# The second layer's attention: products with the values of two units in one chunk, and where the preparations of keys and values stand

## The chip, the cores and the metric

The kernel runs on one core of one Trainium2 chip. The metric is the device time of one execution in microseconds, the median of several runs. A core has five engines that work through queues of their own and wait for each other by semaphores: TensorE (PE in the profile, matmuls and transposes), VectorE (DVE), ScalarE (ACT), GpSimd (POOL) and SyncE (SP, which issues DMAs).

## The reference

The program is a backbone of two layers over 1024 latent tokens and 256 context tokens, 1024 wide. The first layer is windowed attention beside a gated MLP. The second, which matters here, is latent attention with 16 heads: queries from a rank of 256, keys and values from a rank of 128, a rotary part of 32 shared by all heads' keys, and a gate.

```python
def mla_keys_values(kv_a, k_pe, kv_norm, w_kvb, row, col):
    kv = (rms_norm(kv_a, kv_norm) @ w_kvb).reshape(B_, L, C_HEADS, C_NOPE + C_V)
    k_nope, v = kv[..., :C_NOPE], kv[..., C_NOPE:]
    ...
    k = jnp.concatenate([k_nope, jnp.broadcast_to(k_pe, (B_, L, C_HEADS, C_ROPE))], axis=-1)
    return k, v

    ...
    def one(qblk):
        s = jnp.einsum('bqhd,bkhd->bhqk', qblk, k).astype(jnp.float32) * scale
        p = jax.nn.softmax(s, axis=-1).astype(v.dtype)
        return jnp.einsum('bhqk,bkhd->bqhd', p, v)

    ...
    y = (o * jax.nn.silu(gate)) @ w_out
```

All is float32. Each latent token attends to all 1280 tokens.

## The kernel before

The first layer, the second layer's projections and the output products stand before and after the part that changes, and are not touched. In `layer1_attention` the work is cut into 64 units `(hp, qg, e)`: 8 pairs of heads, 4 groups of 256 queries, 2 heads of a pair. The even and the odd unit of the same `hp` and `qg` are the two heads of a pair; their results share one accumulator in PSUM. A loop over n = 0 to 66 runs one step each, and inside a step the list `ORDER1` (line 43) gives the order of the operations by letters. The order of PE, ACT, DVE and POOL is exactly the order in which the program writes them (`manual_schedule`, line 1319); only DMAs on SP are placed by the planner.

What the letters do in step n:

- S0 to S4 (`scores`): scores of unit n, each as three matmuls in a split of float32 in two parts. S0 and S1 fill the two-bank tile s0 (first 128 queries, 1024 keys), S2 and S3 the tile s1 (other 128 queries), S4 the context's 256 keys of both (`sx`).
- X0, X1, X2 (`maxima`, DVE) and P0, P1 (`peak`, DVE): the largest score of each row.
- E0 to E3 (`exponent`, ACT): exponentials and their sums. E0 and E2 are of the first 128 queries, E1 and E3 of the others.
- T0 to T4 (`turn`): transposes of the probabilities of unit n - 1 on PE, four at a time into one bank, and the copy out of that bank: T0 and T3 by DVE, T1, T2 and T4 by ACT (`TURNS`, line 45).
- A0 (`av`, line 1260): products of the transposed probabilities `pt` with the values, for both heads of pair m, keys `k0` to `k1` of ten blocks of 128. The two heads go to the two halves of 64 columns of PE. `AVS` (line 44) says which blocks: in an even step n = 2m + 2 blocks 0 to 4, in the odd step n = 2m + 3 blocks 5 to 9.
- I and U (`inverses`, `inverses_out`): inverses of the sums, turned by PE into the same accumulator, in odd steps. C (`gated`): division and gate of a finished pair, by DVE, in the next even step.
- B and R (`prep_q`, in even steps): at B the queries' projection for the next group on PE, at R the casts to `qh` (ACT) and the subtractions to `ql` (DVE, line 1165) that empty its bank.
- D and L: one stage each of the preparations that `plan` (line 1304) picks for the step, by s = n mod 16: `prep_pair` (keys of the next pair of heads and weights of its queries) in the steps of `PAIR`, `prep_v` (values of the next four heads) in the steps of `VALUES` (line 41). The first step of each loads and splits weights; in the later ones D is the products on PE and L the copies out of PSUM. Keys come in three blocks of columns (512, 512, 256), values in five.

The banks of PSUM set what waits for what. `tm` is two banks in turn (line 1193), for the transposes T, the preparations' products and the queries' projection alike: each of these waits until the operation two before it in that row has been copied out. `acc` is one bank. The transposed probabilities `pt` have three buffers (`PTS`, line 28).

The list of line 43, with the tuples that the change touches:

```python
PAIR, VALUES = (2, 3, 4, 5, 8, 9, 11, 13), (1, 6, 7, 10, 12, 14)
ORDER1 = 'S0 S1 T0 T1 I C X0 S4 S2 X2 P0 T2 T3 E0 E2 S3 T4 D X1 P1 L E3 E1 A0 U B R'.split()
AVS = ((0, 5),), ((5, 10),)
TURNS = 'VAAVA'
```

Of the kernel before, what the change touches and what calls it, by code (L numbers as in the profile page):

```python
# [37 lines left out]
LAGS = 2, 1, 2, 3, 3  # L38
OUT_K = (3, 0, 1, 2, 4, 5, 6, 7)

PAIR, VALUES = (2, 3, 4, 5, 8, 9, 11, 13), (1, 6, 7, 10, 12, 14)
WQ = 'VGG'
ORDER1 = 'S0 S1 T0 T1 I C X0 S4 S2 X2 P0 T2 T3 E0 E2 S3 T4 D X1 P1 L E3 E1 A0 U B R'.split()
AVS = ((0, 5),), ((5, 10),)
TURNS = 'VAAVA'
KPE = {3: [0], 5: [1]}
KPEE = "AV"
# [6 lines left out]
class Kernel:  # L54
# [1116 lines left out]
    def layer1_attention(self):  # L1171
# [70 lines left out]
        def turn(n, a):  # L1242

            if a == 0:
                pts[n] = self.t(pp, [P, NT, QG], F32, "pt")
            tp = self.bank()
            blocks = [(k, j) for k in (8, 9) for j in range(2)] if a == 4 else [(4 * (a % 2) + k, a // 2) for k in range(4)]
            for o, (k, j) in enumerate(blocks):
                nc.tensor.transpose(tp[:, o * P:(o + 1) * P], probs[n][j][:, k * P:(k + 1) * P], self.ident)  # L1249
            if a == 4:  # L1250
                dst, src = pts[n][:, 8:10], tp.rearrange("p (k q) -> p k q", k=2)
            else:
                k, j = blocks[0]
                dst, src = pts[n][:, k:k + 4, j * P:(j + 1) * P], tp.rearrange("p (k q) -> p k q", k=4)
            if TURNS[a] == "A":
                nc.scalar.copy(dst, src)  # L1256
            else:
                nc.vector.tensor_copy(dst, src)  # L1258

        def av(m, k0, k1):  # L1260
            hp, qg, _ = units[2 * m]
            if k0 == 0:
                accs[m] = self.psum("acc")
            for kt in range(k0, k1):
                for e in range(2):
                    vc = ((2 * hp + e) % 4) * 64
                    mm(accs[m][64 * e:64 * e + 64, 0:QG], lhsT=self.v4[hp // 2][:, kt, vc:vc + 64],  # L1267
                       rhs=pts[2 * m + e][:, kt], start=kt == 0, stop=kt == NT - 1)

        def inverses(m):  # L1270

            t = totals.pop(m)
            nc.vector.tensor_tensor(t[:, 2], t[:, 0], t[:, 1], op=ALU.add)
            spread[m] = v = self.t(c2, [P, 2, 2, 64], F32, "spread", bufs=2)
            nc.vector.reciprocal(t[:, 2], t[:, 2])
            nc.gpsimd.tensor_copy(v, t[:, 2].rearrange("p (e j) -> p j e", e=2).unsqueeze(3).broadcast_to([P, 2, 2, 64]))

        def inverses_out(m):

            r = spread.pop(m).rearrange("p j e c -> p j (e c)")  # L1280
            for j in range(2):
                nc.tensor.transpose(accs[m][:, QG + j * P:QG + (j + 1) * P], r[:, j], self.ident)

        def gated(m):

            hp, qg, _ = units[2 * m]
            acc = accs.pop(m)
            cols = slice(qg * QG, (qg + 1) * QG)
            gt = self.t(k2, [P, QG], F32, "gt", bufs=2)
            nc.sync.dma_start(gt, self.g1_d[hp * P:(hp + 1) * P, cols])  # L1290
            nc.vector.scalar_tensor_tensor(gt, acc[:, QG:2 * QG], 0.5, gt, op0=ALU.mult, op1=ALU.mult)
            y = self.t(k2, [P, QG], F32, "y7", bufs=4) if hp == 7 else gt
            nc.vector.tensor_tensor(y, acc[:, 0:QG], gt, op=ALU.mult)
            if hp == 7:
                self.y7[qg] = y
            else:
                nc.sync.dma_start(self.c_d[qg, hp], y)

        def plan_q(n):
            hp, g = n // 8, n % 8 // 2 + 1  # L1300
            hp, g = (hp + 1, 0) if g == 4 else (hp, g)
            return [self.prep_q(hp, g)] if n % 2 == 0 and hp < 8 else []

        def plan(n):
            s, hp = n % 16, n // 8
            if s == 0:
                self.values = self.prep_v(hp // 2 + 1) if hp < 6 else iter(())
            if s % 8 == 0 and hp < 7:
                self.pairs = self.prep_pair(hp + 1)
            out = []  # L1310
            if s in PAIR and hp < 7:
                out.append(self.pairs)
            if s in VALUES:
                out.append(self.values)
            return out
# [3 lines left out]
        with self.tc.manual_schedule(engines={E.PE, E.Activation, E.DVE, E.Pool}):  # L1319
            for n in range(N + 3):  # L1320
                odd = n % 2
                for op in ORDER1:
                    o, a = op[0], int(op[1:] or 0)
                    if o in "SXPE":
                        if n < N:
                            {"S": scores, "X": maxima, "P": peak, "E": exponent}[o](n, a)
                    elif o == "T":
                        if 1 <= n <= N:
                            turn(n - 1, a)
                            if n == N and a in (1, 2, 3):  # L1330
                                next(first)
                    elif o in "AIU":

                        m = (n - 2 - odd) // 2
                        if 0 <= m < N // 2:
                            if o == "A":
                                av(m, *AVS[odd][a])
                            elif odd and o == "I":
                                inverses(m)
                            elif odd:  # L1340
                                inverses_out(m)
                                if n == N + 1:
                                    next(first)
                    elif o == "C":
                        for k in list(accs):
                            if k <= (n - 4) / 2:
                                gated(k)
                    elif o == "B":
                        qs = plan_q(n) if n < N else []
                        for p in qs:  # L1350
                            next(p, None)
                    elif o == "R":
                        for p in qs:
                            next(p, None)
                    elif o == "D":
                        preps = plan(n) if n < N else []
                        for p in preps:
                            next(p, None)
                    elif o == "L":
                        for p in preps:  # L1360
                            next(p, None)
                if n in KPE:
                    self.kpe(1, KPE[n])
                if n == N - 3:
                    self.es_c1t.close()
                    self.es_wx = ExitStack()
                    self.wxp = self.pool(self.es_wx, "wx")
                if n == N - 9:
                    self.wraws = [self.wo1_load(k) for k in OUT_K[:2]]
                elif N - 8 <= n < N:  # L1370
                    self.wo1_split(n - N + 8)
                if n == N - 8:
                    self.out_load(0)
                if n in (N - 4, N - 3, N - 2):
                    self.out_split(0, n - N + 4)
                    if n == N - 2:
                        self.out_load(1)
                if n == N - 1:
                    first = self.out_steps(0)
# [195 lines left out]
```

## Time and profile before

| | us |
|---|---|
| median of 3 runs | 1511.12 (1508.85 to 1515.84) |
| profiled execution | 1512.58, its span 1510.8 |
| PE busy | 1444.1, 96% of the span |
| DVE, ACT, POOL busy | 877.8, 736.9, 399.3 |
| second layer's attention | from 812.6 (first scores) to 1424 (last products with the values) |

The profile is of one execution. A start time is counted from the beginning of the span. Matmuls are pipelined, so the distance from the start of one instruction to the start of the next one on PE says more than its duration. In brackets behind an instruction stands how long its engine was idle before it, and which instruction ended that.

### The profile page before, as it was taken

The numbers are of one execution on the slowest core, as the hardware profiler recorded it, in microseconds if no ns is written. First come the engines' busy times: TensorE is split into PE (matmuls) and PEld (weight loads), VectorE is DVE, ScalarE is ACT, GpSimd is POOL, SyncE is SP. The second block draws the span as 40 slices with busy tenths as digits, with TensorE's granted clock in tenths as the row PEclk, the third lists the DMA queues.
The fourth block names the chain that finished last, engine by engine and source line by source line (L and its number), as shares of the span: only waits on it lengthen the run. The fifth ranks groups of instructions, "written<-read, shape, count | busy, mean of one in ns | idle before, by whom it ended". The sixth has DMA issues, their size and how long they took to land.

```text
span 1510.8 us, 23163 instructions
## 1 busy us (share of the span) xinstructions
PE 1444.1 (96%) x8849; PEld 1136.9 (75%) x8849; DVE 877.8 (58%) x1690; ACT 736.9 (49%) x1563; POOL 399.3 (26%) x351
## 2 busy tenths in 40 slices
PE   5999999999999799999998999999999999999998
PEld 3766899777666477879887777777777777777786
DVE  5582124356677876633744766676667666766454
ACT  4422310145567644433425766666666666676311
POOL 4243233223556532332371110011001100124100
PEclk9999999999999899999999999999999999999999
DMA  8557401222214636412141000000000000212241
GB/s 331 221 221 273 134 29 29 89 77 87 71 42 148 186 112 183 147 64 67 49 139 47 17 24 19 22 26 23 18 25 24 24 15 22 71 47 76 99 147 70
DMA packets 83783, 132.64 MB, mean 88 GB/s; under 512 B 7552, under 2 KB 59976, under 8 KB 80600
## 3 DMA queue, kind: packets, MB, share of 16 engines
q1 hardware_dynamic: 83528, 130.91, 25.6%
q8 instruction: 69, 1.13, 0.3%
q14 instruction: 42, 0.34, 0.1%
q10 hardware_dynamic: 144, 0.26, 0.0%
HBM read 99.59 MB, written 31.56 MB: 87 GB/s over the span
## 4 chain that ended last, share of the span: by engine, by line
PE 78%; DVE 10%; DMA 4%; ACT 3%; issue 3%; POOL 1%; SPq 0%; POOLq 0%; ACTq 0%; DVEq 0%
PE acc L1267 9%; PE s L101 7%; PE s L100 7%; PE s L102 7%; PE tm L1249 7%; PE b L100 5%; PE b L101 4%; PE b L102 4%; PE s L1212 3%; PE s L1213 3%; PE s L1214 3%; PE tm L100 2%; PE acc L772 2%; DVE peak L1224 2%; DMA yf<-y_d 2%
## 5 line engine op out<-in xcount | busy, mean ns | idle before, releaser
L1256 ACT COPY pt<-tm 128x512 f32<-128x512 f32 x192 | 112.4, 585 | 165.9 <-PE tm L1249 165.9
L1249 PE MATMUL tm<-ident,prob 128*128 128x128 f32 x1280 | 178.3, 273 | 8.6 <-DVE ql L1165 2.2
L1249 PEld LDWEIGHTS tm<-ident,prob 128*128 128x128 f32 x1280 | 150.8, 140 | 42.7 <-PE tm L1249 9.5
L1239 ACT ACTIVATE prob<-s,peak 128x1024 f32<-128x1024 f32 x128 | 143.3, 1119 | 37.7 <-DVE peak L1228 34.0
L1224 DVE TENSOR_REDUCE peak<-s 128x1 f32<-128x1024 f32 x128 | 155.0, 1211 | 3.2 <-PE s L1214 3.2
L1267 PE MATMUL acc<-pt,v 128*64 128x256 f32 x1280 | 152.0, 384 | 0.0
L96 POOL TENSOR_TENSOR ql<-pe,qh 32x512 fp32r<-32x512 f32 x32 | 40.7, 1270 | 414.4 <-ACT qh L88 386.2
L1258 DVE COPY pt<-tm 128x512 f32<-128x512 f32 x128 | 87.8, 686 | 79.6 <-PE tm L1249 77.6
L96 POOL TENSOR_TENSOR w_lo<-raw,w_hi 128x512 fp32r<-128x512 f32 (+1 forms) x60 | 75.3, 1269 | 199.9 <-DVE w_hi L90 98.4
L1267 PEld LDWEIGHTS acc<-pt,v 128*64 128x64 f32 x1280 | 86.3, 136 | 49.7 <-issue 9.6
L1212 PE MATMUL s<-kh,qh 96*128 96x512 f32 x256 | 109.5, 428 | 1.8 <-DVE raw L186 1.5
L1213 PE MATMUL s<-kl,qh 96*128 96x512 f32 x256 | 101.3, 396 | 0.0
L1214 PE MATMUL s<-kh,ql 96*128 96x512 f32 x256 | 101.2, 395 | 0.0
L1165 DVE TENSOR_TENSOR ql<-tm,qh 64x256 fp32r<-64x256 f32 x62 | 26.1, 421 | 83.7 <-ACT qh L1163 83.2
L100 PE MATMUL b<-h,yh 128*128 128x512 f32 x160 | 64.1, 400 | 3.1 <-ACT b L884 3.1
L100 PE MATMUL s<-h,w_hi 128*128 128x512 f32 x160 | 63.8, 412 | 2.5 <-ACT qk L380 2.2
L101 PE MATMUL s<-h,w_hi 128*128 128x512 f32 x160 | 64.2, 401 | 0.4 <-DVE h L96 0.4
L102 PE MATMUL s<-h,w_lo 128*128 128x512 f32 x160 | 63.2, 396 | 0.0
L101 PE MATMUL b<-h,yh 128*128 128x512 f32 x160 | 63.0, 394 | 0.0
L102 PE MATMUL b<-h,yl 128*128 128x512 f32 x160 | 62.8, 393 | 0.0
L1239 ACT ACTIVATE prob<-sx,peak 128x256 f32<-128x256 f32 x128 | 61.0, 477 | 1.8 <-DVE peak L1228 1.2
L1214 PEld LDWEIGHTS s<-kh,ql 96*128 96x128 f32 x256 | 48.3, 189 | 11.2
(468 smaller groups left out, 3746.1 us busy)
## 6 DMA issues: line engine op xcount, KB each, us to landing
wa<-in_w_ada_dram SPq DMA_DIRECT2D x16, 1024.0 KB, 8.4
x<-in_xs_dram SPq DMA_DIRECT2D x20, 512.0 KB, 5.4
raw<-in_w_dram SPq DMA_DIRECT2D x17, 512.0 KB, 3.8
wa<-in_w_adag_dram SPq DMA_DIRECT2D x8, 1024.0 KB, 6.5
raw<-in_w_out_dram SPq DMA_DIRECT2D x10, 512.0 KB, 3.3
yf<-y_d SPq DMA_DIRECT2D x10, 512.0 KB, 5.0
x_d<-x SPq DMA_DIRECT2D x8, 512.0 KB, 3.6
raw<-in_w1g_dram SPq DMA_DIRECT2D x8, 512.0 KB, 3.5
```

What stands on the lines that cost most here:

```text
L96: e.tensor_tensor(lo, src, hi.bitcast(F32), op=ALU.subtract)
L100: mm(out, lhsT=ah, rhs=bh, start=start, stop=False)
L101: mm(out, lhsT=ah, rhs=bl, start=False, stop=False)
L102: mm(out, lhsT=al, rhs=bh, start=False, stop=stop)
L1212: mm(o, lhsT=qh[0:96, q], rhs=kh[0:96, k0:k1], start=True, stop=False)
L1213: mm(o, lhsT=qh[0:96, q], rhs=kl[0:96, k0:k1], start=False, stop=False)
L1214: mm(o, lhsT=ql[0:96, q], rhs=kh[0:96, k0:k1], start=False, stop=True)
L1224: nc.vector.reduce_max(m[:, 0, a:a + 1], banks[n, a], axis=AX.X)
L1239: nc.scalar.activation(probs[n][j][:, TL:T] if c else probs[n][j][:, 0:TL], src, AF.Exp, bias=peaks[n][:, 2, j:j + 1], scale=scale, accum_ ...
L1249: nc.tensor.transpose(tp[:, o * P:(o + 1) * P], probs[n][j][:, k * P:(k + 1) * P], self.ident)
L1256: nc.scalar.copy(dst, src)
L1267: mm(accs[m][64 * e:64 * e + 64, 0:QG], lhsT=self.v4[hp // 2][:, kt, vc:vc + 64], rhs=pts[2 * m + e][:, kt], start=kt == 0, stop=kt == NT - 1)
```

## The change

It replaces three tuples and lets a step hold no chunk of `av` at all. With the new `AVS` an even step has none, and the odd step n = 2m + 3 has all ten blocks of keys for both heads. With the new `PAIR` the four stages of a pair's keys stand at s = 0, 1, 3, 5 and 8, 9, 11, 13; with the new `VALUES` the six stages of the values stand at s = 2, 3, 5, 7, 9, 11. The stages at s = 0, 2 and 8 load and split weights; all those with products are odd. In s = 3, 5, 9 and 11 both preparations have products, the keys first.

```diff
-PAIR, VALUES = (2, 3, 4, 5, 8, 9, 11, 13), (1, 6, 7, 10, 12, 14)
+PAIR, VALUES = (0, 1, 3, 5, 8, 9, 11, 13), (2, 3, 5, 7, 9, 11)
...
-AVS = ((0, 5),), ((5, 10),)
+AVS = (), ((0, 10),)
...
                             if o == "A":
-                                av(m, *AVS[odd][a])
+                                for ks in AVS[odd][a:a + 1]:
+                                    av(m, *ks)
```

## Rows read from the trace of the kernel before

**Rows 1.** page: engines' busy time; the chain that ended last, by engine

```profile
PE 1444.1 (96%) x8849; PEld 1136.9 (75%) x8849; DVE 877.8 (58%) x1690; ACT 736.9 (49%) x1563; POOL 399.3 (26%) x351
...
PE 78%; DVE 10%; DMA 4%; ACT 3%; issue 3%; POOL 1%; SPq 0%; POOLq 0%; ACTq 0%; DVEq 0%
```

**Rows 2.** timeline of PE, n = 16, 17 (start, duration, engine, line)

```profile
960.04 0.48 PE L1212 MATMUL s<-kh,qh 96*128 96x512 f32 x1
...
965.37 0.60 PE L1249 MATMUL tm<-ident,prob 128*128 128x128 f32 x4
...
965.90 2.38 PE L1267 MATMUL acc<-pt,v 128*64 128x256 f32 x20
...
968.21 0.38 PE L100 MATMUL tm<-qnh,w_hi 128*128 128x256 f32 x1
...
969.00 0.40 PE L1212 MATMUL s<-kh,qh 96*128 96x512 f32 x1
...
970.38 1.38 PE L1249 MATMUL tm<-ident,prob 128*128 128x128 f32 x8
...
971.52 0.36 PE L1212 MATMUL sx<-kh,qh 96*128 96x256 f32 x1
...
977.62 0.48 PE L1212 MATMUL s<-kh,qh 96*128 96x512 f32 x1
```

**Rows 3.** timeline of DVE, same steps: T3's copy, ql

```profile
965.52 0.68 DVE L1258 COPY pt<-tm 128x512 f32<-128x512 f32 x1
...
970.13 0.86 DVE L1165 TENSOR_TENSOR ql<-tm,qh 64x256 fp32r<-64x256 f32 x2 [2.54 <-ACT qh L1163]
```

**Rows 4.** timeline of ACT, same steps: E1, casts of qh

```profile
968.21 1.13 ACT L1239 ACTIVATE prob<-s,peak 128x1024 f32<-128x1024 f32 x1
...
969.29 0.75 ACT L1163 CAST qh<-tm 64x256 fp32r<-64x256 f32 x2
```

**Rows 5.** timeline of PE: first scores of n = 32; last `av`

```profile
1110.39 0.48 PE L1212 MATMUL s<-kh,qh 96*128 96x512 f32 x1
...
1419.77 4.54 PE L1267 MATMUL acc<-pt,v 128*64 128x256 f32 x40
```

**Rows 6.** timeline of PE: T1 of n = 1

```profile
822.71 0.63 PE L1249 MATMUL tm<-ident,prob 128*128 128x128 f32 x4 [2.24 <-DVE ql L1165]
```

**Rows 7.** timeline of PE, n = 10 and 11, with preparations

```profile
908.75 0.39 PE L100 MATMUL tm<-wvh,kvh 128*128 128x256 f32 x1 [0.29 <-DVE pt L1258]
...
909.66 2.38 PE L1267 MATMUL acc<-pt,v 128*64 128x256 f32 x20
...
918.31 0.60 PE L1249 MATMUL tm<-ident,prob 128*128 128x128 f32 x4
918.67 0.50 PE L100 MATMUL tm<-kvh,w_hi 128*128 128x512 f32 x1
...
919.55 2.38 PE L1267 MATMUL acc<-pt,v 128*64 128x256 f32 x20
```

**Rows 8.** timeline of DVE, n = 10: T3's copy

```profile
908.02 0.68 DVE L1258 COPY pt<-tm 128x512 f32<-128x512 f32 x1
```

**Rows 9.** timeline of ACT, n = 11: T4's copy

```profile
919.66 0.58 ACT L1256 COPY pt<-tm 128x512 f32<-128x512 f32 x1
```

**Rows 10.** DMA view, attention: count, KB each, us to landing

```profile
raw<-in_wq_n_dram SPq DMA_DIRECT2D x6, 128.0 KB, 2.0
```

**Rows 11.** timeline of PE: two instructions behind waits

```profile
469.95 1.12 PE L721 MATMUL tm<-ident,mx 128*128 128x128 f32 x4 [2.40 <-DVE mx L715]
...
812.63 0.50 PE L1212 MATMUL s<-kh,qh 96*128 96x512 f32 x1 [1.47 <-DVE raw L186]
```

**Rows 12.** windows: PE, PEld, DVE, ACT, POOL busy; PEclk; DMA; GB/s

```profile
471.00:472.00 1.00, 1.00 (x5) 0.48 (x3) 0.01 (x1) 1.00 (x4) 0.92 (x1) 0.50 1.06 414
...
814.50:817.60 3.10, 3.10 (x11) 2.56 (x10) 1.85 (x3) 1.06 (x2) 0.00 (x0) 0.50 0.10 32
823.00:826.00 3.00, 3.00 (x24) 2.73 (x22) 2.56 (x5) 1.33 (x3) 0.72 (x1) 1.00 0.08 22
```

## The prediction

> **What bounds the kernel now.** I read the page first. TensorE (PE) is busy for 96% of the span and owns 78% of the chain that ended last [rows 1], so one wants to count PE's work alone. The change, however, touches only the 64 steps of the second layer's attention, so its worth must be read from one pair of steps there. I took the pair n = 16, 17, in which no products of the preparations run. On PE it goes from the first scores at 960.04 to the next even step's at 977.62, 17.58 us [rows 2]. I then put VectorE (DVE) and ScalarE (ACT) beside it, to see what PE's order has to keep up with [rows 3, 4].
>
> What the reader should see is a chain that PE's busy share hides. The transposes T0 to T4, the products of the preparations and the queries' projection (`prep_q`, op B) share the two `tm` banks, so each waits until the operation two before it has been copied out. The projection of an even step is followed by T0 and T1 of the odd step, so T1 waits for the copies of the queries. Those come late on their engines: ACT first does E1 (from 968.21), then the casts of qh (969.29, right behind) [rows 4]; DVE's subtractions of ql end at 970.13 + 0.86 = 970.99 [rows 3]; the odd step's T1 can start only then, and S4 follows at 971.52 [rows 2]. The chain up to there (maximum over the second half of the scores, peak, E3, E1, qh, ql) starts from S3 and T3, which lie ahead of the products with the values (`av`). So in an even step the 2.31 us from 965.90 to 968.21 in which PE works on `av` [rows 2] lie beside that chain and cost almost nothing.
>
> **The change part by part.** It does three things to PE's order.
>
> First, the even half of `av` moves to the odd step. In the even step what follows T4 is now the projection. It takes the bank that T3 used, so it waits for DVE's copy of T3, which starts at 965.52 [rows 3]; in another step the next product on that bank started 0.73 after the copy did [rows 7, 8]; so 966.25. It lasts 0.79 (968.21 to 969.00), the scores S0 and S1 then 1.38 (969.00 to 970.38) [rows 2], and T0 some 0.36, so PE is ready for T1 at 968.8. The bank is free at 970.99 as before, because nothing ahead of that in ACT's or DVE's queue has moved. PE stands still for about 2.2 us, and the odd step's S4 starts at 971.52 in the new order as in the old: the removal saves nothing here. The trace has such a step already: in n = 0 and 1 there is no `av` yet, and T1 of n = 1 waited 2.24 us for ql [rows 6].
>
> In the odd step `av` doubles. At the end of the attention, where both halves happen to stand together, forty products last 4.54, against 2.38 for twenty [rows 2, 5]: 2.16 more, and on PE's own path, for behind S4 the odd step is PE work without a wait. A pair without preparations becomes 17.58 + 2.16 = 19.74 us. There are 31 such pairs (the first has no `av`). In the last steps the projection is missing, but S0 of n = 63 waits for E0 of n = 62 anyway, so I count that pair alike.
>
> Second, the preparations' products gather in odd steps: keys in s = 1, 3, 5, 9, 11, 13, values in s = 3, 5, 7, 9, 11 (s is n mod 16). Taken from rows, each adds to 19.74: a block of keys of 512 columns (919.55 - 918.31) - (965.90 - 965.37) = 0.71; one of 256 columns half of that, an estimate, 0.36; values alone 0.36 (918.31 to 918.67) + 0.91 (908.75 to 909.66) - 0.53 = 0.74 [rows 2, 7]. Where both stand in one step the values' products take T4's bank, and T4 is copied by ACT only behind E0 and E2. That copy starts at 919.66, 1.35 after T4 did, and lasts 0.58 [rows 7, 9], so they start at 920.29 and `av` at 921.20; without preparations it would be 918.84: 2.36 together, of which 0.8 is standing still. This happens four times in sixteen steps.
>
> Third, the loading steps move: keys to s = 0, values to s = 2. The DMAs of the raw weights, on SP's queue, land 2.0 us after their issue [rows 10], and their buffer is free since the split of the weights before, two steps earlier at least; the attention's other loads and stores, which they are moved past, are issued once or twice in a step. I take no time for them; a load that comes late would hold DVE at the split, in front of ql, and be added in full to T1's wait, three times 2.0 us in sixteen steps, which I leave out as excluded by that lead. The cast of the values' weights lands ahead of E3 in an even step and lengthens the chain there. Its bounds are nothing and the 0.75 of the pair of qh casts [rows 4]; I take half, 0.37.
>
> Sixteen steps then take, pair by pair, 20.45 + 22.47 + 22.10 + 20.48 + 22.10 + 22.10 + 20.10 + 19.74 = 169.5 us. Before, they took 1110.39 - 960.04 = 150.35 [rows 2, 5]: 19.2 more. The third sixteen are the same; the first lack one `av`, 17.0; the last (no values, fewer keys) I count at 8 x 2.16 = 17.3. The sum is **72.7 us**. Against the profiled execution, which took 1512.58, that makes 1585.
>
> **What the waits do to PE's clock.** The trace shows that a wait of PE can cost more than itself. After a wait of 1.47 us ahead of 812.63 the granted clock was 0.50 for 3.1 us, the lower of the two levels, 1.2 instead of 2.4 GHz; after one of 2.40 us ahead of 469.95 too; after the one of 2.24 us of n = 1 it stayed at 1.00 [rows 6, 11, 12]. The new order has 31 waits of 2.2 us, none of which is there now. One drop costs half of 3.1 us, 1.55, because PE is the bound behind it. The bounds are none of 31 (0 us) and all (48 us); with the two waits nearest in length one each way, I take half, 15 x 1.55 = 23 us. That gives 1608 for the profiled execution; the median of the runs, 1511.12, lies 1.5 below it, so I predict 1607 us.
>
> A rule of the Trainium skill speaks for the higher end. Its page "TensorE: Matmul & The Clock Gate", section "A second HAM failure mode: psum-queue depth-cycling", says that PE pausing briefly between groups of matmuls, as PSUM banks are cycled, makes the clock go back and forth between its levels, and that throughput suffers. By it alone all 31 waits would pay, and the time would be 1632. The rows agree for two of the three waits.
>
> **The rivals.** (1) The waits are there, and the clock never falls: 1584. For it speaks the wait of n = 1 [rows 6, 12]. All of them fall: 1632. Both belong to the forecast's mechanism and are the ends of its range.
>
> (2) Faster. If the cover by `av` isn't needed, PE's work alone decides. Then a pair saves what the change of shape costs: entering `av` from the transposes 0.53 - 0.36 [rows 2, 7] and ending it once instead of twice, 2 x 2.31 - 4.47 (4.54 less the 0.07 by which 2.38 exceeds 2.31) [rows 2, 5], 0.32 together, and the 0.3 that T1 waits now: 31 x 0.6 = 20 us, 1491. It decides for this if the queries are copied out by the time at which T0 ends, 2.2 us earlier than E1's place in ACT's queue allows [rows 4]. Against it stands the wait in n = 1 [rows 6].
>
> The section "Key Properties" of the Trainium skill's "TensorEngine Tiling (Array Packing)" favours this rival: a change between tiling modes drains the engine, and the new order changes mode half as often. The rows show such a price, the 0.32 above, which is small.
>
> (3) No change within 0.5%: the wait at T1 exists but is short, since something in ACT's queue of the even step (the values' copy is gone from it) moves E1 forward. In n = 16 that copy was absent already, and the chain was the one computed. That the order isn't what the change says is no more likely: the order of PE, ACT and DVE is written out by hand.
>
> **How the numbers follow.** The forecast with its clock variants has 0.94, faster 0.03, no change 0.03. The mechanism without drops (1584) less 4 us for the values' weights and the merged end of `av`, and the one with all drops (1632) plus as much, bound the range: 1580 to 1636. Half a percent is about what a measurement of this kernel can tell from no change.
>
> **What would show it.** In the profile after: `av` as groups of forty products in odd steps only; a wait of about 2.2 us of PE on `tm`, released by ql (L1165), some 31 times, against one now; about a dozen waits of 0.8 us on ACT's copy ahead of the values' products; a pair without preparations at 19.7 us or, with a drop, some 21.3; a granted clock of the attention clearly under 0.98. My forecast is wrong if T1 of the odd step starts right behind T0, or if S4 of the odd step comes earlier than 11.5 us after the even step's first scores.

## The result, and the profile after

The changed kernel takes 1611.12 us (median of 6 runs, 1597.12 to 1619.35) against 1510.5 (1508.85 to 1515.84): a ratio of 1.0657, 95% interval 1.0622 to 1.0692. It is slower by 100.6 us. The profiled execution took 1611.12, its span 1609.3.

The page of the kernel after, PE's line of part 1 and the engines' line of part 4, which answer [rows 1]:

```profile
PE 1475.6 (92%) x8849; PEld 1169.9 (73%) x8849; DVE 883.7 (55%) x1690; ACT 736.2 (46%) x1563; POOL 398.8 (25%) x351
...
PE 59%; DVE 13%; issue 11%; ACT 10%; DMA 3%; POOL 2%; SPq 0%; ACTq 0%; DVEq 0%; POOLq 0%
```

The work is the same, 8849 matmuls, and PE is even busy for 31 us more, part of it at the lower clock (below). But its share of the chain that ended last fell from 78 to 59%, and DVE, ACT and "issue" took it over. So PE now waits for others. The list of PE's waits in the kernel after names them (who waited for whom: us in all, times, longest):

```profile
PE tm L1249 <- DVE ql L1165: 63.8, 31, 2.4
...
PE tm L100 <- DVE pt L1258: 8.7, 29, 0.4
PE tm L100 <- ACT pt L1256: 6.3, 10, 1.0
```

The first line stood at 2.2 us, once, before [rows 6]. The second is the projection, behind DVE's copy of T3, and the third the values' products, behind ACT's copy of T4.

Here is PE's timeline of a pair without products of the preparations, n = 30 and 31, in the kernel after; it answers [rows 2]:

```profile
1134.96 0.48 PE L1212 MATMUL s<-kh,qh 96*128 96x512 f32 x1
...
1140.29 0.60 PE L1249 MATMUL tm<-ident,prob 128*128 128x128 f32 x4
...
1141.17 0.39 PE L100 MATMUL tm<-qnh,w_hi 128*128 128x256 f32 x1 [0.29 <-DVE pt L1258]
...
1143.38 0.60 PE L1249 MATMUL tm<-ident,prob 128*128 128x128 f32 x4
1146.05 0.63 PE L1249 MATMUL tm<-ident,prob 128*128 128x128 f32 x4 [2.07 <-DVE ql L1165]
1146.43 0.36 PE L1212 MATMUL sx<-kh,qh 96*128 96x256 f32 x1
...
1150.03 4.54 PE L1267 MATMUL acc<-pt,v 128*64 128x256 f32 x40
1154.50 0.44 PE L1282 MATMUL acc<-ident,spread 128*128 128x128 f32 x2
1154.70 0.48 PE L1212 MATMUL s<-kh,qh 96*128 96x512 f32 x1
```

And DVE's timeline of the same pair, which answers [rows 3]:

```profile
1145.05 0.85 DVE L1165 TENSOR_TENSOR ql<-tm,qh 64x256 fp32r<-64x256 f32 x2 [2.55 <-ACT qh L1163]
```

Read it from T4 (1140.29). The projection follows behind a wait of 0.29 us for T3's copy (1141.17), where `av` stood before; T0 of the odd step (1143.38) comes 2.7 us ahead of T1 (1146.05), and T1 starts 0.15 us after ql has ended (1145.05 + 0.85). S4 of the odd step comes 11.47 us after the even step's first scores; before, it was 971.52 - 960.04 = 11.48 [rows 2]. Taking 2.3 us of PE work out of the even step brought nothing at all. The odd step has forty products in one piece, and the pair takes 1154.70 - 1134.96 = 19.74 us instead of 17.58.

Other pairs in the kernel after, by windows from one pair's first scores to the next pair's (columns as in [rows 12]):

```profile
980.32:1002.33 22.01, 19.66 (x130) 15.56 (x129) 13.58 (x25) 12.12 (x27) 2.39 (x3) 0.92 0.08 25
...
1134.96:1154.70 19.74, 17.39 (x127) 13.77 (x126) 11.31 (x20) 10.97 (x25) 1.67 (x2) 1.00 0.06 17
1154.70:1178.24 23.54, 21.19 (x130) 16.87 (x129) 13.58 (x25) 12.34 (x27) 2.39 (x3) 0.85 0.07 23
```

The first and the last hold the same work, a pair with one block of keys, and take 22.01 and 23.54 us, at a mean granted clock of 0.92 and 0.85. The sum of the prediction gave such a pair 20.45 without a fall of the clock. In the first of the two, the clock fell right behind the wait for ql, first its line in PE's timeline, then the windows around it:

```profile
991.41 0.98 PE L1249 MATMUL tm<-ident,prob 128*128 128x128 f32 x4 [2.06 <-DVE ql L1165]
```

```profile
982.00:990.00 8.00, 7.06 (x48) 5.91 (x46) 5.96 (x12) 5.16 (x13) 0.73 (x1) 1.00 0.16 49
992.50:996.00 3.50, 3.50 (x19) 3.06 (x19) 2.17 (x5) 1.02 (x2) 0.40 (x1) 0.65 0.06 19
996.00:999.50 3.50, 3.50 (x28) 2.37 (x28) 2.22 (x4) 3.44 (x9) 0.00 (x0) 1.00 0.00 0
```

### The profile page after: what moved, and what is told of

Same layout as the page of the kernel before. It is cut to its first block, busy times and chain, and to the rows that moved or that the text cites. A ratio compares the mean times of both kernels' runs of the same rounds, so it can differ in the third digit from the quotient of the medians.

```text
span 1609.3 us, 23148 instructions
## 1 busy us (share of the span) xinstructions
PE 1475.6 (92%) x8849; PEld 1169.9 (73%) x8849; DVE 883.7 (55%) x1690; ACT 736.2 (46%) x1563; POOL 398.8 (25%) x351
## 4 chain that ended last, share of the span: by engine, by line
PE 59%; DVE 13%; issue 11%; ACT 10%; DMA 3%; POOL 2%; SPq 0%; ACTq 0%; DVEq 0%; POOLq 0%
PE acc L1267 7%; ACT prob L1239 6%; PE s L100 6%; PE s L101 6%; PE s L102 6%; PE b L100 4%; PE b L101 4%; PE b L102 4%; PE tm L1249 4%; DVE peak L1224 2%; PE acc L772 2%; DVE ql L1165 2%; PE s L1212 1%; PE s L1213 1%; PE s L1214 1%
## 5 line engine op out<-in xcount | busy, mean ns | idle before, releaser
L1249 PE MATMUL tm<-ident,prob 128*128 128x128 f32 x1280 | 192.3, 288 | 65.9 <-DVE ql L1165 63.8
L1249 PEld LDWEIGHTS tm<-ident,prob 128*128 128x128 f32 x1280 | 164.3, 149 | 103.0 <-issue 76.4
L1267 PE MATMUL acc<-pt,v 128*64 128x256 f32 x1280 | 145.2, 382 | 0.0
L1212 PE MATMUL s<-kh,qh 96*128 96x512 f32 x256 | 115.5, 451 | 3.7 <-ACT prob L1239 2.2
L1213 PE MATMUL s<-kl,qh 96*128 96x512 f32 x256 | 106.1, 415 | 0.0
L1214 PE MATMUL s<-kh,ql 96*128 96x512 f32 x256 | 106.0, 414 | 0.0
```

Of the source, the lines that this page charges most:

```text
L1212: mm(o, lhsT=qh[0:96, q], rhs=kh[0:96, k0:k1], start=True, stop=False)
L1213: mm(o, lhsT=qh[0:96, q], rhs=kl[0:96, k0:k1], start=False, stop=False)
L1214: mm(o, lhsT=ql[0:96, q], rhs=kh[0:96, k0:k1], start=False, stop=True)
```

## The experiments

The theory: in an even step `av` covered PE's wait for the queries' copies; moved away, PE stands still for some 2 us in every pair, does the moved work later at full price, and loses its clock on top. The rivals: the gathered preparations are the cost; merging the two chunks is itself the cost; the clock costs nothing; PE's own work decides.

### The two parts of the change, one at a time

The new `AVS` with the old preparations, as an edit of the changed kernel:

```diff
-PAIR, VALUES = (0, 1, 3, 5, 8, 9, 11, 13), (2, 3, 5, 7, 9, 11)
+PAIR, VALUES = (2, 3, 4, 5, 8, 9, 11, 13), (1, 6, 7, 10, 12, 14)
```

> The new AVS alone, with the old PAIR and VALUES. Theory (the even step loses the cover of T1's wait for the queries' copies): T1 of the odd step still waits for ql wherever an even step has no products of a preparation, and less behind those that have; sixteen steps take about 165 us instead of 150 before and 169 after, which without falls of the clock makes some 54 us, with falls 80 to 90: 1590 to 1600. Rival (the gathering of the preparations in odd steps is the cost): 1511 to 1520.

It took 1580.95 us, ratio 1.0447 (1.0417 to 1.0477). Its waits of PE:

```profile
PE tm L1249 <- DVE ql L1165: 45.9, 31, 2.1
```

The preparations alone, in the kernel before:

```diff
-PAIR, VALUES = (2, 3, 4, 5, 8, 9, 11, 13), (1, 6, 7, 10, 12, 14)
+PAIR, VALUES = (0, 1, 3, 5, 8, 9, 11, 13), (2, 3, 5, 7, 9, 11)
```

> The new PAIR and VALUES alone, with av in two halves as before. Theory: sixteen steps take 152 us instead of 150, most of it the values' products waiting 0.8 us for ACT's copy of T4 in s = 3, 5, 9 and 11: 1515 to 1520, no wait for ql. Rival (the gathering is the cost): 1570 or more.

It took 1516.49 us, ratio 1.0031 (1.0020 to 1.0042). Its waits of PE:

```profile
PE tm L100 <- ACT pt L1256: 9.0, 12, 1.0
...
PE tm L1249 <- DVE ql L1165: 2.8, 5, 1.5
```

In the kernel before, the list has no such waits on ACT's copy, but shorter ones on DVE's, which are gone here:

```profile
PE tm L100 <- DVE pt L1258: 4.9, 16, 0.4
```

So the preparations alone cost 5 us, about what the twelve waits add (9.0 us) less these sixteen (4.9), and the move of `av` alone 69. That rules the gathering out as the main cost. The run with the new `AVS` alone, 1580.95, lies below what I had expected, 1590 to 1600. The steps went as expected: the sixteen from n = 16 on took 166.15 us, with one fall of the clock among them, where I had put down about 165. It was the clock that fell less often than I had put in. The parts don't add up to the 100 us of the whole, 26 are missing: with the old `PAIR` and `VALUES`, even steps hold products of the preparations too, and these fill part of the wait, 45.9 us in all instead of 63.8. The clock falls less often then: read in steps of 0.25 us, and with a stretch of double length counted twice, the attention has 12 falls in the run with the new `AVS` alone and 22 in the changed kernel. Ten falls at some 1.55 us each are the larger part of the 26. The new places take this last cover away.

### The same merge in the other step

```diff
-AVS = (), ((0, 10),)
+AVS = ((0, 10),), ()
```

> All of av in the even step instead of the odd one, the preparations as in the changed kernel. It merges the same two chunks. Theory (what counts is the cover between T4 and the odd step's T1): the 4.5 us of av stand ahead of the queries' projection, T1 waits 0.3 us at most, but S0 of the even step now waits about 0.5 us for E0 of the odd step where the odd step has no products; sixteen steps take about 150 us: 1505 to 1518, granted clock 0.99. Rival (merging the chunks is itself the cost, by the longer hold of acc or a longer run on PE): as slow as the changed kernel, about 1611.

It took 1520.01 us, ratio 1.0052 (1.0033 to 1.0072). PE's timeline around the pair n = 30, 31:

```profile
1096.54 0.63 PE L1249 MATMUL tm<-ident,prob 128*128 128x128 f32 x4 [0.46 <-DVE kl L1144]
...
1100.53 4.54 PE L1267 MATMUL acc<-pt,v 128*64 128x256 f32 x40
1104.99 0.39 PE L100 MATMUL tm<-qnh,w_hi 128*128 128x256 f32 x1
...
1107.18 1.35 PE L1249 MATMUL tm<-ident,prob 128*128 128x128 f32 x8
...
1112.40 0.50 PE L1212 MATMUL s<-kh,qh 96*128 96x512 f32 x1 [0.25 <-ACT prob L1239]
```

Forty products in one piece cost little by themselves: the same merge with the same preparations, one step earlier, takes 91 us less than the changed kernel and 3.5 us more than the run with the preparations alone. T0 and T1 of the odd step stand together again (1107.18, 1.35 for eight, as in [rows 2]). The rival of the merge falls. My range was 2 us too low: I had seen the wait of the scores for E0 (0.25 here), not that T1 of an even step can wait for the keys' subtractions (kl, 0.46 here, nine times in all), which stand late in DVE's queue.

### The work put back as a filler

```diff
...
                                 for ks in AVS[odd][a:a + 1]:
                                     av(m, *ks)
+                                if not odd and n < N:
+                                    filler(m)
```

> The changed kernel with 20 products more on PE (half a pair's av over again, into acc, result unused) in the place in the even step from which av was taken; 2.3 us of PE work more per pair, some 71 us in all. Theory (PE only waits there, and the clock falls after the waits): the work fills the wait, T1's wait for ql shrinks to 0.3 us or less, and the falls of the clock vanish: 1575 to 1585, faster than the changed kernel although it computes more. Rival (the waits alone are the cost and the clock costs nothing): 1605 to 1615. Rival (PE's work is the bound): 1680.

It took 1582.91 us, ratio 1.0468 (1.0439 to 1.0498). PE does 20 products more per pair, and the kernel is 28 us faster than the changed one. So the rivals that the clock costs nothing (1605 to 1615) and that PE's own work decides (1680) fall. Two of its pairs by windows, n = 16, 17 with a block of keys and n = 30, 31 without, and its wait for ql, of which seven are left:

```profile
978.98:999.42 20.44, 20.29 (x150) 15.53 (x149) 13.31 (x25) 12.12 (x27) 2.41 (x3) 1.00 0.09 26
1128.58:1148.32 19.74, 19.60 (x147) 15.10 (x146) 11.30 (x20) 10.97 (x25) 1.67 (x2) 1.00 0.06 17
```

```profile
PE tm L1249 <- DVE ql L1165: 4.0, 7, 2.3
```

This takes the two costs apart. The pair n = 30, 31 is 19.74 us here and in the changed kernel alike: PE either works for these 2 us or stands still, and the next step starts at the same time. The pair n = 16, 17 takes 20.44 with the filler, at a clock of 1.00, against 22.01 at 0.92. Over the thirty pairs from n = 2 on, nineteen of the changed kernel are longer than those with the filler by over 0.4 us, most of them by about 1.55 or twice that, together with the rest 30.5 us. That is the price of the clock. What is left, 1582.91 - 1511.22 = 72 us, is the price of the order.

### Where the wait goes when the bank is freed

The queries' projection goes to the bank `acc`, which nothing holds between C of an even step and `av` of the odd one:

```diff
...
-        tp = self.bank()
+        tp = self.qbank()
...
+        self.qbank = lambda: self.psum("acc")
```

> The changed kernel, but the queries' projection goes to the bank acc, which is empty from C of an even step to av of the odd one; nothing else moves. Theory (the wait is for the bank that the queries' copies empty): T1's wait for ql is gone; the next limit is T2, which waits about 1.1 us for DVE's copy of T0, queued behind ql. A pair is 1.2 to 1.4 us shorter, 40 us, and the waits are too short for most falls of the clock, another 15 to 30: 1540 to 1560. Rival (ACT and DVE are themselves too late, whatever the bank): PE waits 2 us in other places, 1600 or more.

It took 1585.22 us, ratio 1.0494 (1.0474 to 1.0515), which is 25 us above the range I had given. Most of the 26 us that it gains on the changed kernel is the clock's: counted as above, there are 8 falls instead of 22, and 14 at 1.55 us make 22 us. PE's timeline, first scores of an odd step, T2 and T3 of it, and the keys' products of an odd step twelve microseconds earlier:

```profile
957.36 0.38 PE L100 MATMUL tm<-kvh,w_hi 128*128 128x256 f32 x1 [1.35 <-DVE pt L1262]
...
969.52 0.50 PE L1216 MATMUL s<-kh,qh 96*128 96x512 f32 x1 [0.30 <-ACT prob L1243]
...
973.88 1.09 PE L1253 MATMUL tm<-ident,prob 128*128 128x128 f32 x8 [0.42 <-ACT pt L1260]
```

and DVE's timeline of the same step:

```profile
972.66 0.85 DVE L1168 TENSOR_TENSOR ql<-acc,qh 64x256 fp32r<-64x256 f32 x2 [2.54 <-ACT qh L1166]
973.55 0.69 DVE L1262 COPY pt<-tm 128x512 f32<-128x512 f32 x1
```

T1 no longer waits for ql. But DVE still does ql ahead of the copy of T0, and ACT qh ahead of that of T1. A pair without preparations gains 1.6 us (18.13 instead of 19.74); one with a block of keys takes 20.43, against 20.44 with the filler, so nothing at all: the delay runs on through DVE's queue to the copy of T3, and the keys' products wait for it, 1.35 us. My expectation had stopped at the first wait behind. If this is right, the queries' copies must go behind the copies of the transposes. This run has the edit of the last one and moves R, with B in even steps only:

```diff
-... 'S0 S1 T0 T1 I C X0 S4 S2 X2 P0 T2 T3 E0 E2 S3 T4 D X1 P1 L E3 E1 A0 U B R'
+... 'S0 S1 T0 T1 I C X0 S4 S2 X2 P0 T2 T3 R E0 E2 S3 T4 D X1 P1 L E3 E1 A0 U B'
...
-                        qs = plan_q(n) if n < N else []
-                        for p in qs:
-                            next(p, None)
+                        if not odd:
+                            qs = plan_q(n) if n < N else []
+                            for p in qs:
+                                next(p, None)
...
-                        for p in qs:
+                        for p in qs if odd else []:
```

> The changed kernel with the queries' projection in acc, as in the run e4, and the copies of the queries (R) moved from the end of the even step to behind T3 in the odd step, so that they stand behind the copies of T0 to T3 in ACT's and DVE's queues. Theory (in e4 the queries' copies still stood ahead of T0's and T3's copies, and their delay came back as the keys' products waiting 1.35 us): the keys' products wait 0.4 us, sixteen steps take about 158 us instead of 169, with av waiting about 1 us for ql where a step has no products: 1535 to 1555 with few falls of the clock. Rival (the copies' place in the queues doesn't matter): 1585 as e4.

It took 1546.69 us, ratio 1.0234 (1.0215 to 1.0254). A pair with one block of keys is at 18.24 us instead of 20.43, and one without preparations about as long. Its waits of PE:

```profile
PE tm L100 <- ACT pt L1260: 22.9, 12, 2.2
...
PE acc L1271 <- DVE ql L1168: 7.6, 11, 2.1
```

The attention has 8 falls of the clock here too, so the 38.5 us gained on the last run are not the clock's: it was the place in the two queues, with the bank only as the messenger. The price shows as well: ACT now does the queries' casts ahead of E0, T4's copy comes later, and the values' products wait 1.9 us for it instead of 0.8.

### The length of the chain

In the changed kernel the gating of the finished pair, 0.8 us of DVE ahead of X0, goes behind P1:

```diff
-... 'S0 S1 T0 T1 I C X0 S4 S2 X2 P0 T2 T3 E0 E2 S3 T4 D X1 P1 L E3 E1 A0 U B R'
+... 'S0 S1 T0 T1 I X0 S4 S2 X2 P0 T2 T3 E0 E2 S3 T4 D X1 P1 C L E3 E1 A0 U B R'
```

> The changed kernel with the gating C behind P1 instead of ahead of X0 (in the changed kernel acc is not needed again before the odd step); 0.8 us of DVE's work leave the chain, nothing is added. Theory (the chain of DVE and ACT from the scores to ql is what T1 waits for): S4 of every odd step comes 0.75 us earlier, 31 x 0.75 = 23 us; the wait itself stays near 1.9 us since the projection starts earlier too, so the clock falls about as often: 1580 to 1595. Rival (only the place of av matters, DVE's queue doesn't): 1611.

It took 1588.19 us, ratio 1.0525 (1.0495 to 1.0556), 23 us less than the changed kernel. Its wait for ql:

```profile
PE tm L1249 <- DVE ql L1165: 62.3, 31, 2.1
```

The wait is about as long as in the changed kernel, yet the odd steps come earlier: where the clock stays up, a pair without preparations takes 19.14 us instead of 19.74 and one with a block of keys 19.84 instead of 20.44, 0.6 less, a little under the 0.75 that I had put down. The projection isn't held up by T3's copy any more (the changed kernel's 29 waits for it, 8.7 us, are gone from the list), so T1 starts to wait earlier and is also released earlier. The sum of a wait in the list is no measure of what it costs. And the kernel before, with a shorter chain in even steps, by another place of C and by T3's copy on ACT:

```diff
-ORDER1 = 'S0 S1 T0 T1 I C X0 S4 S2 X2 P0 T2 T3 E0 E2 S3 T4 D X1 P1 L E3 E1 A0 U B R'.split()
+ORDER1 = 'S0 S1 T0 T1 I X0 S4 S2 X2 P0 C T2 T3 E0 E2 S3 T4 D X1 P1 L E3 E1 A0 U B R'.split()
...
-TURNS = 'VAAVA'
+TURNS = 'VAAAA', 'VAAVA'
...
-            if TURNS[a] == "A":
+            if TURNS[(n + 1) % 2][a] == "A":
```

> The kernel before, with a shorter way from the scores to the queries' copies in even steps: the gating of the finished pair (C, 0.8 us of DVE) stands behind P0 instead of ahead of X0, and T3 of an even step is copied by ACT, which is idle there, instead of DVE. Theory (the chain over DVE's and ACT's queues ends in T1, whoever covers it): the values' products in even steps no longer wait 0.5 us for T3's copy, and the 0.3 us that T1 waits are gone; 3 to 3.5 us in sixteen steps: 1497 to 1504. Rival (PE's own work is the bound before, the chain is hidden): 1511, no change.

It took 1504.66 us (median of 5 runs, 1500.93 to 1506.71), ratio 0.9949 (0.9929 to 0.9968). This is faster than both kernels, by some 8 us against the kernel before, and just outside the range I had given. Half of the expectation held. The values' products in even steps start without a wait, and pairs that have them are 0.6 us shorter (n = 10, 11: 18.93 us instead of 19.51). But T1 still waits its 0.3 us: a pair without preparations takes 17.53 us, where it took 17.58. PE's timeline of n = 16, 17 (first scores, projection's first and last product, S0, T0 and T1 of the odd step) and ACT's (E1, the reading of its sums, casts of qh):

```profile
954.50 0.48 PE L1212 MATMUL s<-kh,qh 96*128 96x512 f32 x1
...
962.66 0.38 PE L100 MATMUL tm<-qnh,w_hi 128*128 128x256 f32 x1
...
963.34 0.28 PE L102 MATMUL tm<-qnh,w_lo 128*128 128x256 f32 x1
963.45 0.40 PE L1212 MATMUL s<-kh,qh 96*128 96x512 f32 x1
...
964.84 1.34 PE L1249 MATMUL tm<-ident,prob 128*128 128x128 f32 x8
```

```profile
962.33 1.16 ACT L1239 ACTIVATE prob<-s,peak 128x1024 f32<-128x1024 f32 x1
963.33 0.24 ACT L1239 ACTIVATION_READ_ACCUMULATOR prob<-s,peak 128x1 f32 x1
963.71 0.75 ACT L1163 CAST qh<-tm 64x256 fp32r<-64x256 f32 x2
```

E1 with its sums (963.33 + 0.24) and the projection (963.34 + 0.28) end together, and qh starts behind both (963.71); the casts and subtractions alone then take longer than S0, S1 and T0. The chain is also less short than I meant it to be: E1 starts 962.33 - 954.50 = 7.83 us into the pair, before 968.21 - 960.04 = 8.17 [rows 2, 4], so 0.34 us earlier and not the 0.8 of C's work, since ACT now copies T3 ahead of E0. With `av` as cover the projection's end is the next limit, and shortening the chain alone gains next to nothing there.

## Why the prediction was right

It said 1607 us, 1580 to 1636, for the reason that the trace then showed. Point by point:

- **T1's wait.** About 2.2 us, released by ql, some 31 times, is 2.06 us on average, 31 times. S4 of the odd step didn't move, 11.47 against 11.48.
- **The pairs.** 19.74 us predicted without preparations, 19.74 measured. With the filler, where the clock stays up, the eight pairs of n = 16 to 31 measure 20.44, 22.39, 22.05, 20.44, 22.09, 22.08, 20.11 and 19.74, where the sum had 20.45, 22.47, 22.10, 20.48, 22.10, 22.10, 20.10 and 19.74: 169.3 against 169.5 us.
- **The order's price.** 72.7 us predicted; 72 by the filler's run, which has its own first pair and end, so that the agreement is better than the measurement of either.
- **The values' products behind T4's copy.** Twelve waits of 0.8 us were predicted. The run with the preparations alone shows twelve, 0.75 on average; the changed kernel itself has ten, 0.63 on average.
- **The clock.** This term was too small. I took 15 falls at 1.55 us, 23 us; the run with the filler shows 28 us, the sum over pairs 30.5. The single price was right, the number of falls was near 20. Taking half of the waits was a choice between two bounds, with one row for either, so that the sum came within 4 us of the measured time is in part luck; the runs of the changed kernel alone differ by 22 us.
- **The chain.** I described it as starting from S3 and the maximum X1. The rows of ACT show it starts earlier: from E0 on, ACT works without a gap through E2, T4's copy, E3 and E1 to the casts of qh, and E0 waits for P0 (E0 and the casts of qh of the pair n = 30, 31 in the kernel after stand below). That is why C's place ahead of X0 counts, as the changed kernel with C moved shows. The end of the chain, and with it the sum, was the same.

```profile
1140.64 1.12 ACT L1239 ACTIVATE prob<-s,peak 128x1024 f32<-128x1024 f32 x1 [0.70 <-DVE peak L1228]
...
1144.21 0.75 ACT L1163 CAST qh<-tm 64x256 fp32r<-64x256 f32 x2
```

The rival "faster" is dead by the change itself, and the one that puts the cost into the preparations by its own run. Forty products did take 4.47 us to the next instruction (1150.03 to 1154.50) instead of twice 2.31, 0.15 less, in a pair that lost 2.16. The Trainium skill's page "TensorEngine Tiling (Array Packing)", section "Key Properties", has a change between tiling modes drain the engine, and half as many changes were made here; whether the 0.15 us are such a drain, no run shows.

What stays open: which of the waits are followed by a fall of the clock. In the changed kernel 19 of 31 were, with nearly the same wait in each pair.

## What to carry to other kernels

Before work is moved out of a step, look for what PE would do in its place: here work that lay beside a chain of other engines was free there, and cost its whole time behind the chain. Follow the chain through the queues, not through the bank that PE happens to wait for: freeing the bank moved the wait to the next copy behind it, and only moving the copies in the queues made a pair with a block of keys shorter. When a wait of 2 us appears in every round of a loop, count the clock as well: here it added 28 us to 72.

## What the runs showed of the hardware

Waits of 2.06 us of PE, one in some 20 us of otherwise dense work, were followed 19 times in 31 by a fall of the granted clock to its lower level of 1.2 GHz: the mean over the attention fell to 0.94, and each fall cost about 1.55 us. Adding 20 products per pair, whose results nobody used, kept the clock up and made the kernel 28 us faster. The Trainium skill's page "TensorE: Matmul & The Clock Gate", section "A second HAM failure mode: psum-queue depth-cycling", tells of such going back and forth through short idle times of PE; this case agrees with it and adds a price.
